# Shortening the first load of a DMA-bound max-pooling kernel from 8 KB to 2 KB per partition

## Chip, cores and metric

One core of one Trainium2 chip. The metric is the device time of one execution in microseconds (us); the span in a profile is about 1.8 us shorter.

The time of the kernel before was 335.2 us, the median of three runs (335.18 to 335.23).

## The reference

The input is 32 x 256 x 4096 fp32 (134.2 MB). Every window of 16 neighbours becomes its maximum; the output is 32 x 256 x 256 fp32 (8.4 MB).

```python
def reference(x, output_size):                 # x: (32, 256, 4096), output_size 256
    batch, channels, length = x.shape
    result = np.zeros((batch, channels, output_size), dtype=np.float32)
    for i in range(output_size):
        start = int(i * length / output_size)
        end = int((i + 1) * length / output_size)
        result[:, :, i] = np.max(x[:, :, start:end], axis=-1)
    return result
```

## The kernel before

The 2,097,152 windows are spread evenly: 16,384 to each of 128 partitions. They are loaded in pieces into three slots that are used in turn; VectorE reduces each piece. All results stay on chip in the same area, growing down from its top, so the slots must shrink as the results grow. The pieces form three groups. Within a group every partition has one contiguous row in HBM, and each group has its store; the last is cut in two.

```python
    AREA = 53200          # fp32 elements of a partition
    SLOTS = 3
    MOST = 65536 // (4 * W)      # 1024 windows: 64 KB of a partition; W = 16
    ALIGN = 4
    FIRST = 128           # windows of a partition in the first load
    ROUNDS_A = 3
    LAST = 4

    slot_sizes = [MOST]
    rounds = [[FIRST] + [MOST] * (SLOTS - 1)]
    left = total - sum(rounds[0])
    while left:
        room = AREA - (total - left)
        n = min(room // (SLOTS * W + SLOTS) // ALIGN * ALIGN, MOST)
        ...                                             # cut: fills `rounds`
    sizes = [n for r in rounds for n in r]
    groups = [sizes[:1], sizes[1 : ROUNDS_A * SLOTS], sizes[ROUNDS_A * SLOTS :]]
    ...                                                 # cut: views of input and output
        for i, size in enumerate(loads):
            a = b - size
            at = n_loads % SLOTS * slot_sizes[n_loads // SLOTS] * W
            slot = area[:, at : at + size * W]
            nc.sync.dma_start(out=slot, in_=xg[:, a * W : b * W])
            nc.vector.reduce_max(
                out=area[:, base + a : base + b],
                in_=slot.rearrange("p (n w) -> p n w", w=W),
                axis=mybir.AxisListType.X,
            )
            n_loads += 1
            b = a
    ...                                                 # cut: collects `stores`
    for dst, src in stores[1:2] + stores[0:1] + stores[2:]:
        nc.sync.dma_start(out=dst, in_=src)
```

So there are 20 loads and 4 stores, all issued in order by SyncE. The first three loads wait for nothing; each later load waits until the reduce of its slot's previous content has ended. The stores are, in order: second group, first group, most of the third group, and last the results of the last four reduces.

Of the kernel before, what the change touches and what calls it, by code (L numbers as in the profile page):

```python
# [1 line left out]

# [4 lines left out]


@with_exitstack
def kernel(  # L10
    ctx: ExitStack,
    tc: tile.TileContext,
    x: bass.AP,
    output_size: bass.AP,
    out: bass.AP,
):






    nc = tc.nc
    P = nc.NUM_PARTITIONS
    fp32 = mybir.dt.float32

    B, C, L = x.shape
    O = int(output_size)
    assert L % O == 0, (L, O)
    W = L // O  # L30
    total = B * C * O // P
    assert B * C * O % P == 0

    AREA = 53200
    SLOTS = 3
    MOST = 65536 // (4 * W)
    ALIGN = 4
    FIRST = 128
    ROUNDS_A = 3
    LAST = 4  # L40

# [7 lines that stand above are left out]
        if left <= slot_sizes[-1]:  # L49
            n = left  # L50
        slot_sizes.append(n)
        rounds.append([])
        while left and len(rounds[-1]) < SLOTS:
            n = min(n, left)
            rounds[-1].append(n)
            left -= n
    sizes = [n for r in rounds for n in r]
    groups = [sizes[:1], sizes[1 : ROUNDS_A * SLOTS], sizes[ROUNDS_A * SLOTS :]]

    pool = ctx.enter_context(tc.tile_pool(name="pool", bufs=1))  # L60
    area = pool.tile([P, AREA], fp32, tag="area", name="area")

    xw = x.flatten_outer_dims().rearrange("r (o w) -> (r o) w", w=W)
    ow = out.flatten_outer_dims().rearrange("r o -> (r o)")

    stores = []
    n_loads = 0
    first = 0
    low = AREA
    for g, loads in enumerate(groups):  # L70
        n = sum(loads)
        xg = xw[first : first + P * n].rearrange("(p n) w -> p (n w)", p=P)
        og = ow[first : first + P * n].rearrange("(p n) -> p n", p=P)
        first += P * n
        base = low - n
        b = n
# [12 lines that stand above are left out]
        low = base  # L89
        if g < len(groups) - 1:  # L90
            stores.append((og, area[:, base : base + n]))
        else:
            end = sum(loads[len(loads) - LAST :])
            for a, b in ((end, n), (0, end)):
                stores.append((og[:, a:b], area[:, base + a : base + b]))

    for dst, src in stores[1:2] + stores[0:1] + stores[2:]:
        nc.sync.dma_start(out=dst, in_=src)


# [1 line left out]
_INS = ['x', 'output_size']  # L102
_OUTS = [((32, 256, 256), 'float32')]

_NUMBERS = {'output_size': 256}


# [26 lines left out]
```

## Time and profile before

| What | Value | Where it is read |
|---|---|---|
| time, span | 335.2 us, 333.4 us | run times, page |
| DMA engines busy | 99.2% | queue section of the page |
| VectorE busy | 276.0 us (83%) | page, part 1 |
| VectorE's waits, all for loads | 49.2 us | view of waits |
| rate of 64 KB packets, one engine | 27.08 GB/s (2.42 us each) | packet records of the trace |

From the page of the kernel before:

```profile
span 333.4 us, 113 instructions
DVE 276.0 (83%) x20; POOL 0.2 (0%) x4
...
DMA packets 3456, 142.61 MB, mean 428 GB/s; under 512 B 384, under 2 KB 512, under 8 KB 512
...
q1 hardware_dynamic: 3456, 142.61, 99.2%
...
DMA 64%; DVE 31%; DVEq 1%; another core or an unknown queue 0%; SPq 0%; issue 0%
```

The line of queue q1 says that this one queue kept 16 engines busy for 99.2% of the span. The last line, the chain of waits, credits VectorE with 31%; a chain that meets a reduce just before a load's issue counts the reduce, even if the engines have another load queued meanwhile. The view of waits has, for VectorE (us in total, times, longest):

```profile
DVE area L82 <- DMA area<-in_x_dram: 49.2, 19, 17.1
```

The timeline of the kernel before (start us, duration, engine, line, operation, output<-input with shapes, count, and in brackets the idle time before and what ended it):

```profile
5.60 2.29 DVE L82 TENSOR_REDUCE area<-area 128x128 f32<-128x2048 f32 x1 [5.60 <-DMA area<-in_x_dram]
24.95 17.22 DVE L82 TENSOR_REDUCE area<-area 128x1024 f32<-128x16384 f32 x1 [17.06 <-DMA area<-in_x_dram]
44.30 17.22 DVE L82 TENSOR_REDUCE area<-area 128x1024 f32<-128x16384 f32 x1 [2.13 <-DMA area<-in_x_dram]
...
296.18 13.22 DVE L82 TENSOR_REDUCE area<-area 128x784 f32<-128x12544 f32 x1 [1.61 <-DMA area<-in_x_dram]
310.18 15.01 DVE L82 TENSOR_REDUCE area<-area 128x736 f32<-128x11776 f32 x2 [0.78 <-DMA area<-in_x_dram]
```

A reduce starts when its load has landed, and a load has landed when all of the 16 engines are done. The last line covers the last two reduces; they end at 310.18 + 15.01 = 325.19 us, when the last store can be issued.

### The profile page before, as it was taken

The numbers are of one execution on the slowest core, as the hardware profiler recorded it, in microseconds if no ns is written. First come the engines' busy times: TensorE is split into PE (matmuls) and PEld (weight loads), VectorE is DVE, ScalarE is ACT, GpSimd is POOL, SyncE is SP. The second block draws the span as 40 slices with busy tenths as digits, with TensorE's granted clock in tenths as the row PEclk, the third lists the DMA queues.
The fourth block names the chain that finished last, engine by engine and source line by source line (L and its number), as shares of the span: only waits on it lengthen the run. The fifth ranks groups of instructions, "written<-read, shape, count | busy, mean of one in ns | idle before, by whom it ended". The sixth has DMA issues, their size and how long they took to land.

```text
span 333.4 us, 113 instructions
## 1 busy us (share of the span) xinstructions
DVE 276.0 (83%) x20; POOL 0.2 (0%) x4
## 2 busy tenths in 40 slices
DVE  2009979797988989797989797989898898989990
POOL 0000000000000000000000000000000000000000
DMA  9898989898989998999999999999999999999997
GB/s 377 377 503 377 503 369 491 369 491 369 491 369 462 462 462 346 462 462 441 434 434 434 434 434 415 409 409 505 415 409 433 433 433 433 433 416 452 391 432 333
DMA packets 3456, 142.61 MB, mean 428 GB/s; under 512 B 384, under 2 KB 512, under 8 KB 512
## 3 DMA queue, kind: packets, MB, share of 16 engines
q1 hardware_dynamic: 3456, 142.61, 99.2%
HBM read 134.22 MB, written 8.39 MB: 428 GB/s over the span
## 4 chain that ended last, share of the span: by engine, by line
DMA 64%; DVE 31%; DVEq 1%; another core or an unknown queue 0%; SPq 0%; issue 0%
DMA area<-in_x_dram 64%; DVE area L82 31%; DVEq L129 1%; SPq L81 0%; DVEq L82 0%
## 5 line engine op out<-in xcount | busy, mean ns | idle before, releaser
L82 DVE TENSOR_REDUCE area<-area 128x1000 f32<-128x16000 f32 (+8 forms) x20 | 276.0, 13806 | 49.2 <-DMA area<-in_x_dram 49.2
L115 POOL MEMSET const-bfloat16-1.0<- 128x1 bf16 x1 | 0.1, 102 | 0.0
L115 POOL MEMSET const-uint8-127<- 128x1 uint8 x1 | 0.1, 102 | 0.0
L115 POOL MEMSET const-float32-0.0<- 128x1 f32 x1 | 0.1, 99 | 0.2 <-issue 0.2
L115 POOL MEMSET const-float32-1.0<- 128x1 f32 x1 | 0.1, 99 | 0.0
## 6 DMA issues: line engine op xcount, KB each, us to landing
area<-in_x_dram SPq DMA_DIRECT2D x3, 8000.0 KB, 39.9
area<-in_x_dram SPq DMA_DIRECT2D x3, 7520.0 KB, 37.5
area<-in_x_dram SPq DMA_DIRECT2D x3, 7072.0 KB, 35.3
area<-in_x_dram SPq DMA_DIRECT2D x3, 6656.0 KB, 33.2
area<-in_x_dram SPq DMA_DIRECT2D x3, 6272.0 KB, 31.3
area<-in_x_dram SPq DMA_DIRECT2D x1, 5888.0 KB, 30.3
out_dram<-area SPq DMA_DIRECT2D x1, 3934.0 KB, 27.4
out_dram<-area SPq DMA_DIRECT2D x1, 2966.0 KB, 33.7
```

The costliest lines, as they stand in the source:

```text
L82: nc.vector.reduce_max(out=area[:, base + a : base + b], in_=slot.rearrange("p (n w) -> p n w", w=W), axis=mybir.AxisListType.X,)
L115: nc = _bacc.Bacc("TRN2", target_bir_lowering=False, num_devices=1)
L129: with _tile.TileContext(nc) as tc:
```

## The change

The intent: the first load exists to give VectorE something early and to stagger the slots. A smaller one starts VectorE sooner and reads one contiguous quarter of a megabyte.

```diff
-    FIRST = 128
+    FIRST = 32
```

The arithmetic of the sizes moves the other 96 windows of each partition into the third group:

| | before | after |
|---|---|---|
| first load, elements of a partition | 2048 | 512 |
| third group's reduces, windows | 884 x3, 832 x3, 784 x3, 736, 152 | 888 x3, 836 x3, 784 x3, 740, 220 |
| first group's store, bytes of a partition | 512 | 128 |
| last two stores, elements of a partition | 5932, 2456 | 5956, 2528 |

The numbers of loads, stores and packets, and all bytes in total, stay the same.

## The prediction

> **What bounds the kernel now.** The DMA queue. The queue section of the page has 99.2% of 16 engines' span, 142.61 MB at 428 GB/s. The trace's DMA packet records show no gap from the first data packet (1.75 us into the span) to the last (332.1 us): 64 KB packets run at 27.08 GB/s per engine, and every load starts as the one before it ends. Outside that stream lie 1.7 us of start and 1.3 us of completion. VectorE is busy 276.0 us (83%); its 49.2 us of waits are all for loads (view of waits). The chain of waits names VectorE for 31%, but each load is issued with another one still queued ahead of it, so this costs nothing.
>
> **What the change does.** Total bytes, loads (20), stores (4) and packets stay. First load 2048 to 512 elements per partition, first reduce 128 to 32 windows; the 96 windows go into the third group: 884 to 888, 832 to 836 (three loads each), 736 to 740, the last 152 to 220. Stores: 128 to 32 windows (512 B to 128 B per partition), 5932 to 5956, 2456 to 2528.
>
> - First load: 8 packets per engine at 0.309 us become about 0.08 us each (estimate: 2 KB at 27.08 GB/s plus the few ns by which 8 KB packets exceed that rate): 1.8 us less. The later loads carry that: 1.8 us more. Net nil. The start-up of about 0.7 us (first packets take about 1 us, not 0.309) stays. The second load is issued 0.43 us after the first, which occupies the engines 0.6 us plus start-up: no hole.
> - Fourth load: issued at about 5 us instead of 7.9; worth nothing, as loads are queued until 44 us.
> - VectorE: a reduce fits 0.155 us + 1.041 ns per element of a partition. First 2.29 to 0.69 us; last 2.68 to 3.8; last but one 12.42 to 12.49.
> - Tail, the only place for a new wait: the last store is issued when the last reduce ends, 325.2 us, and its packets follow the third store's at 328.9 us without a gap; with about 1 us from issue to packets, some 2.5 us are slack. After: the last but one load lands about 1.3 us earlier (68 windows less before it), the two reduces take 1.2 us more: the last ends at 325.2 again.
> - Small store: now 0.2 to 0.3 us between its neighbours. The Trainium skill, "DMA: Bandwidth & Descriptors", Specifications, says that transfers under 512 B do a read-modify-write; nothing here shows it yet. Estimate: -0.1 to +0.3 us.
>
> On the critical path, nothing above 0.3 us changes.
>
> **Predicted: 335.2 us, 80% range 334.8 to 335.7. Faster by over 2%: 0.01; within 2%: 0.98; slower by over 2%: 0.01.**
>
> **What would show each step.** First reduce starts at about 3.8 us instead of 5.6; later reduces through the 784s 1.3 to 1.9 us earlier; the last ends at 325.2 within 0.3; DMA share stays 99%; 2 KB packets take 0.08 us once started; the third store's last packet and the fourth's first still touch.
>
> **What would make it wrong.** A hole at the start, if the second load's descriptors come after the short load's data end. 128 B store packets costing far more than 27 ns each. The third group's row pitch in HBM goes from 536,832 to 542,976 bytes: the same page (Latency and other measured facts) reports low rates at a 512 KiB pitch, restored by a few KiB more; before runs 12.25 KiB above that at full rate, after would run 18.25 KiB above, so I expect no loss, unproven here. The last reduce ending over 2 us late, which would expose the last store.

## The result, and the profile after

| | median us | range | runs |
|---|---|---|---|
| before | 335.19 | 335.16 to 335.23 | 6 |
| after | 335.56 | 335.24 to 335.85 | 6 |

The ratio is 1.001 (95% interval 0.9997 to 1.0023): the same within 2%, and inside the predicted range. A residue of some 0.4 us remains, and the runs scatter more than those of the kernel before.

The page of the kernel after (its profiled run took 335.85 us, the slowest of the six):

```profile
span 334.1 us, 113 instructions
DVE 276.0 (83%) x20; POOL 0.2 (0%) x4
...
DMA packets 3457, 142.61 MB, mean 427 GB/s; under 512 B 513, under 2 KB 513, under 8 KB 641
...
q1 hardware_dynamic: 3456, 142.61, 99.0%
...
DMA 64%; DVE 31%; DVEq 1%; another core or an unknown queue 0%; SPq 0%; issue 0%
```

Its timeline:

```profile
3.44 0.69 DVE L82 TENSOR_REDUCE area<-area 128x32 f32<-128x512 f32 x1 [3.44 <-DMA area<-in_x_dram]
23.76 17.22 DVE L82 TENSOR_REDUCE area<-area 128x1024 f32<-128x16384 f32 x1 [19.64 <-DMA area<-in_x_dram]
43.11 17.22 DVE L82 TENSOR_REDUCE area<-area 128x1024 f32<-128x16384 f32 x1 [2.13 <-DMA area<-in_x_dram]
...
295.43 13.22 DVE L82 TENSOR_REDUCE area<-area 128x784 f32<-128x12544 f32 x1 [1.61 <-DMA area<-in_x_dram]
309.51 16.21 DVE L82 TENSOR_REDUCE area<-area 128x740 f32<-128x11840 f32 x2 [0.86 <-DMA area<-in_x_dram]
```

VectorE does the same work in the same time (276.0 us), and its waits are 49.7 us instead of 49.2:

```profile
DVE area L82 <- DMA area<-in_x_dram: 49.7, 19, 19.6
```

The first reduce starts 2.16 us earlier, but the second only 1.19 us earlier, although the load ahead of it became 8 x 6144 B / 27.08 GB/s = 1.82 us shorter on every engine. So 0.63 us were lost between the first and the second landing. From the second reduce to the third the distance is 19.35 us in both kernels: nothing more is lost there. The last reduce ends at 309.51 + 16.21 = 325.72 us, 0.53 us later than before.

**Where the 0.63 us went.** The trace's packet records show it. In the kernel before, the first 64 KB packet of every engine took 2.42 us, like all later ones. In the kernel after these sixteen packets took 2.82 us on average, and one took 3.60 us. I define an engine's *lag* as follows: the time from the first data packet of the kernel to the end of that engine's last 64 KB packet, less what the same packets take at the steady rate (2.420 us for each 64 KB packet, and size / 27.08 GB/s + 5 ns for each packet of the first load). The 64 KB packets are those of the two full-size loads.

| | mean lag of 16 engines | lag of the slowest | fastest to slowest |
|---|---|---|---|
| before | 0.72 us | 0.91 us | 0.39 us |
| after | 0.88 us | 1.62 us | 1.06 us |

The excess arose in the long packets: when the first 64 KB packet of each engine began, the slowest engine lagged 0.73 us in the kernel after and 0.97 us in the kernel before. The other engines did not make the lag up: at the end of the kernel the engines' last data packets still end 1.04 us apart, against 0.44 us in the kernel before.

### The profile page after: what moved, and what is told of

It reads as the page before. It is cut to its first block, busy times and chain, and to the rows that moved or that the text cites. A ratio compares the mean times of both kernels' runs of the same rounds, so it can differ in the third digit from the quotient of the medians. Undisturbed runs are those within 1.5% of the kernel's fastest.

```text
span 334.1 us, 113 instructions
## 1 busy us (share of the span) xinstructions
DVE 276.0 (83%) x20; POOL 0.2 (0%) x4
## 4 chain that ended last, share of the span: by engine, by line
DMA 64%; DVE 31%; DVEq 1%; another core or an unknown queue 0%; SPq 0%; issue 0%
DMA area<-in_x_dram 64%; DVE area L82 31%; DVEq L129 1%; SPq L81 0%; DVEq L82 0%
## 5 line engine op out<-in xcount | busy, mean ns | idle before, releaser
L82 DVE TENSOR_REDUCE area<-area 128x1000 f32<-128x16000 f32 (+8 forms) x20 | 276.0, 13806 | 49.7 <-DMA area<-in_x_dram 49.7
```

What stands on the lines that cost most here:

```text
L82: nc.vector.reduce_max(out=area[:, base + a : base + b], in_=slot.rearrange("p (n w) -> p n w", w=W), axis=mybir.AxisListType.X,)
```

## The experiments

First theory, START: the residue arises in the first microseconds and the slowest engine carries it to the end. Its rival, REST: the residue comes from what the change did elsewhere, that is from the third group's new addresses or the 128 B store packets. All twelve kernels gave correct results, all in five rounds, on several chips; the kernel before was 335.1 to 335.5 us in every one of its runs beside them (medians 335.19 to 335.27). Diffs are against the changed kernel unless said otherwise.

### after_again: the changed kernel once more

No edit.

> The changed kernel unaltered, as a control for the small residue (335.56 us against 335.19, six runs each). If the residue is real: median 335.4 to 335.7 with runs spread over more than 0.3 us, where the kernel before stays within 0.1 us; and in the trace at least one of the second load's first sixteen 64 KB packets takes over 2.9 us instead of 2.42. If it was an accident of the first series: median 335.2 and a spread under 0.1 us.

Measured: 335.63 us (335.55 to 335.73, 5 runs) against 335.21 (335.11 to 335.29); ratio 1.0013, interval 1.0 to 1.0025. The longest first 64 KB packet took 3.28 us, the mean was 2.77. So the residue of 0.4 us came back and the two ranges do not overlap; the spread was smaller than expected, 0.18 us. I take it as real, and about a tenth of a per cent, though the interval just touches 1.

### short_fourth: the short load in the fourth place

```diff
-        for i, size in enumerate(loads):
-            ... load and reduce in group order ...
+    # pieces are collected first, then loaded and reduced in this order
+    for xg, base, a, b in state[1:4] + state[0:1] + state[4:]:
```

> The short load moves from first to fourth place; sizes, row pitches, stores and the 128 B packets stay as in the changed kernel. Theory START (the residue arises in the first microseconds, where the second load's 64 KB packets follow the short load's 2 KB packets before the engines run steadily, and the slowest engine keeps its lag to the end): median 335.1 to 335.3, spread under 0.15 us. Rival REST (the residue comes from the third group's new addresses or from the 128 B store packets): median 335.4 to 335.7 as in the changed kernel. Both expect VectorE's first reduce at about 22 us and no loss from that.

Measured: 337.89 us (337.59 to 338.20), slower than both expectations. I had built a new hole. The timeline of this kernel:

```profile
42.44 17.22 DVE L94 TENSOR_REDUCE area<-area 128x1024 f32<-128x16384 f32 x1 [2.10 <-DMA area<-in_x_dram]
61.35 17.41 DVE L94 TENSOR_REDUCE area<-area 128x1000 f32<-128x16000 f32 x2 [1.70 <-DMA area<-in_x_dram]
82.94 16.82 DVE L94 TENSOR_REDUCE area<-area 128x1000 f32<-128x16000 f32 x1 [4.18 <-DMA area<-in_x_dram]
```

The fifth load may be issued only when the reduce of the first line ends, at 59.66 us. Behind the third load there is now only the short one, 0.67 us of data, so the engines run dry: from 60.85 to 62.0 us only 7 to 14 of 16 engines are active, mostly 11 or 12, and the next reduce waits 4.18 us instead of some 2. The issue, from the timeline of 59 to 63 us:

```profile
59.68 0.33 SPq L93 DMA_DIRECT2D area<-in_x_dram  x1
```

The first packets of this late load (64,000 B) took 3.01 us on average instead of 2.36. So the run did not settle START against REST. But it showed that stretched first packets are not confined to the start of the kernel: they also come with a load that is issued too late in mid-stream.

### short_on_act: the short load from ScalarE's queue

```diff
-            nc.sync.dma_start(out=slot, ...)
+            (nc.scalar if n_loads == 0 else nc.sync).dma_start(out=slot, ...)
```

> Only the short load is issued by ScalarE's queue, so that the first long load no longer waits 0.43 us for the issue before it. Theory START by late issue (the long load's descriptors come after the 2 KB packets are done): the stretch of the first 64 KB packets (2.54 to 3.60 us in the changed kernel, mean 2.79) falls to under 0.15 us and the median to 335.2 or below. If the stretch has another cause than the issue gap, it stays and the median is 335.4 to 335.7. REST also expects 335.4 to 335.7.

Measured: 335.75 us (335.63 to 335.81). The test did not do what I meant. Both issues began in the same 0.01 us, but the packets of the short load came behind the first long packets: they ran from 3.1 us after the first data packet on, one between two long ones, and the last of them ended 21.6 us after it. The long load had become the first, its first packets took 3.09 us on average (2.82 in the kernel after, which the expectation has as 2.79), and the slowest engine lagged 1.58 us. The issue gap alone is thus not tested here.

### short_spread: the same 2 KB, from rows half a megabyte apart

```diff
-    groups = [sizes[:1], sizes[1 : ROUNDS_A * SLOTS], sizes[ROUNDS_A * SLOTS :]]
+    groups = [sizes[: ROUNDS_A * SLOTS], sizes[ROUNDS_A * SLOTS :]]
-            stores.append((og, area[:, base : base + n]))
+            for a, b in ((n - FIRST, n), (0, n - FIRST)):
+                stores.append((og[:, a:b], area[:, base + a : base + b]))
```

> The 2 KB of every partition come from the ends of the second group's rows, about half a megabyte apart, instead of one contiguous quarter megabyte; the small store is scattered likewise. If the contiguous quarter megabyte is what makes the start uneven: median 335.2 and no first 64 KB packet over 2.6 us. If only the size of the packets matters: median 335.4 to 335.7 with stretched first packets as in the changed kernel. REST expects 335.4 to 335.7 as well.

Measured: 335.89 us (335.75 to 335.97), longest first 64 KB packet 3.21 us, slowest engine's lag 1.48 us. The contiguous quarter of a megabyte is not the cause.

### first_16, first_64, first_512: other sizes of the first load

After these runs a second theory was formed, LEAD: a long load that the engines reach too soon after its issue has its first packets stretched, by different amounts on different engines; data queued ahead of it hides this. Its rivals are written in the expectations; one, SMALL, is that small packets at the very start leave the engines uneven, whatever follows.

```diff
-    FIRST = 32
+    FIRST = 16          # in the others 64 and 512
```

> First load of 1 KB per partition: half the lead of the changed kernel. LEAD expects the first 64 KB packets stretched more than there (mean over 2.8 us) and a median of 335.6 to 336.0. SMALL expects about the same as the changed kernel or more. REST (addresses of the third group) has no reason for a trend with the size.

> First load of 4 KB per partition, lead about 1.2 us plus start-up, between the two kernels of the case. LEAD expects first 64 KB packets with a mean between 2.42 and 2.77 us, and a median between those of the two kernels, 335.2 to 335.5.

> First load of 32 KB per partition: the other direction. DMA-bound view: total bytes are the same, so 335.2 again within 0.5 us. LEAD as far as it goes: the first load, longer itself, has no lead and its own first packets are stretched somewhat, so 335.2 to 335.7. If a longer first load cost time by starting VectorE later (first reduce at about 12 us): over 340 us.

Measured: 336.23 us (336.09 to 336.57) with 16 windows, 335.12 us (335.06 to 335.44) with 64, 335.25 us (335.22 to 335.31) with 512. The second reduce in the timelines of first_16 and of first_64, in this order:

```profile
24.12 17.22 DVE L82 TENSOR_REDUCE area<-area 128x1024 f32<-128x16384 f32 x1 [20.82 <-DMA area<-in_x_dram]
```

```profile
23.67 17.22 DVE L82 TENSOR_REDUCE area<-area 128x1024 f32<-128x16384 f32 x1 [18.40 <-DMA area<-in_x_dram]
```

With 64 windows the first load is 1.21 us shorter than with 128 (8 x 4096 B / 27.08 GB/s), and the second reduce starts 1.28 us earlier: nothing is lost. With 16 windows it is 2.12 us shorter, and the second reduce starts only 0.83 us earlier: 1.29 us are lost. The mean of the first 64 KB packets falls from 3.27 us (16 windows) over 2.82 (32) and 2.54 (64) to 2.42 (128). The trend is what LEAD says, though its medians were off: it forecast 335.6 to 336.0 us for 16 windows and 335.2 to 335.5 for 64. REST has no reason for it, and first_512, whose third group has other sizes and addresses again, is back at the time of before. Note that its first reduce starts only at 12.90 us, 7.3 us later than in the kernel before, which costs nothing.

first_64 is not faster than the kernel before: ratio 0.9999, interval 0.9987 to 1.0011. No version here beats both kernels.

### ladder: 2 KB, then 6 KB, then the long loads

Diff against the kernel *before*:

```diff
+            for c, d in ((0, 32), (32, size)) if n_loads == 0 else ((0, size),):
+                part = slot[:, c * W : d * W]
-                nc.sync.dma_start(out=slot, ...); reduce of the slot
+                nc.sync.dma_start(out=part, in_=xg[:, (a + c) * W : (a + d) * W]); reduce of the part
```

> The kernel before with its first load cut in two: 2 KB, then the other 6 KB of every row, then the long loads. New theory LEAD: a long load (64 KB per partition) that the engines reach less than about 2 us after its issue has its first packets stretched and uneven, because its packets are still being handed out; with more data queued ahead nothing is lost. LEAD expects here: the 6 KB packets in between give the lead back, first 64 KB packets 2.42 us (none over 2.6), median 335.1 to 335.4, spread under 0.2 us. Rival SMALL (2 KB packets in the first microsecond leave the engines uneven whatever follows): 335.5 or more and stretched 64 KB packets.

Measured: median 335.82 us (335.76 to 335.89, and one run of 337.27). LEAD was right about the long packets (mean 2.49 us, one of 2.75) and wrong about the time: the slowest engine lagged 1.59 us all the same, and the mean lag rose to 1.19 us. SMALL was right about the time and wrong about the long packets. Here the loss lies ahead of the long packets: in the first 0.9 us of data only about 8 of the 16 engines had a packet at any time (in the kernel after all 16 had one at 0.3 us), and the small packets moved 200 to 280 GB/s in the second microsecond, where the kernel before reached 424. Why half of the engines began late is not shown. LEAD is at best a part of the cause.

### short_second: the short load second, in a slot of its own

```diff
-    rounds = [[FIRST] + [MOST] * (SLOTS - 1)]
+    rounds = [[MOST] * SLOTS]          # the short load lies behind the three slots
+    # order: long, short, long, long; all four are issued at once
```

> The short load comes second, in a slot of its own, so that it and the long load behind it are issued at the start, some 20 us before the engines reach them. LEAD expects: the 2 KB packets at 0.084 us, the 64 KB packets behind them at 2.42 us (none over 2.6), no hole; only the very first long load, which has no lead, is stretched as when the short load went to ScalarE's queue; median 335.5 to 335.9. Rival SMALL/MID (a short load within the stream costs 2 to 3 us by itself, as the fourth place seemed to show with 337.89): median about 337 to 338.

Measured: 335.67 us (335.48 to 335.69). The 2 KB packets took 0.084 us each, and no hole followed. A short load in mid-stream is harmless if the load behind it is issued in time, so most of the 2.7 us that short_fourth lost, 2.2 us against this kernel, came with the late issue. Here a long load is first, its first packets took 3.10 us and the slowest engine lagged 1.37 us.

### third_late: only two loads issued in the first microsecond

```diff
+    for k in [0, 1, 3, 2] + list(range(4, len(state))):   # third and fourth load exchanged
```

> The changed kernel with its third and fourth load exchanged in the order of issue, so that the third issue waits for the first reduce (about 3.4 us after the first issue instead of 0.9 us) and only two loads are handed out in the first microseconds. Theory HANDOUT (the engines run under rate, and unevenly, as long as packets of all the loads issued back to back are being handed out; the cut first load, which made it four such loads, ended with 335.82): first 64 KB packets with a mean under 2.6 us, the engines' last 64 KB ends within 0.6 us of one another, median 335.3 or below. Theory LEAD (the second load itself was issued too shortly before the engines reach it; the third does not matter): mean 2.7 to 2.9 us, ends spread over 0.8 us, median 335.4 to 335.7.

Measured: 338.18 us (336.85 to 338.81). Issuing the third load 2.5 us later did nothing for the first 64 KB packets: mean 2.79 us. By that HANDOUT falls. Its second sign is not as clear: the engines' last 64 KB packets ended 0.62 us apart, between HANDOUT's forecast (under 0.6) and LEAD's (over 0.8), and the slowest engine lagged 1.24 us. The median is no evidence for either: the exchange left the sixth load with a slot that came free too late. Its timeline:

```profile
61.68 17.22 DVE L95 TENSOR_REDUCE area<-area 128x1024 f32<-128x16384 f32 x1 [2.52 <-DMA area<-in_x_dram]
78.93 18.90 SPq L94 DMA_DIRECT2D area<-in_x_dram  x3
80.66 16.82 DVE L95 TENSOR_REDUCE area<-area 128x1000 f32<-128x16000 f32 x1 [1.75 <-DMA area<-in_x_dram]
102.18 16.82 DVE L95 TENSOR_REDUCE area<-area 128x1000 f32<-128x16000 f32 x1 [4.71 <-DMA area<-in_x_dram]
```

SyncE issues again only at 78.93 us, when the reduce of the first line ends. The engines run dry (at 79.85 us only 4 of 16 are active), the sixteen first packets of this load took 3.28 us on average instead of 2.36, and the reduce after it waits 4.71 us.

### tail_half and tail_full: more VectorE work at the end

These test the prediction's slack at the end, and the 31% of the chain of waits. The last reduce (220 windows), or half of it, is done a second time before the last store.

```diff
+            if n_loads == len(sizes) - 1:
+                nc.vector.reduce_max(
+                    out=area[:, base + a : base + a + h],        # h = size // 2, or size
+                    in_=slot[:, : h * W].rearrange("p (n w) -> p n w", w=W), ...)
```

> The changed kernel with the first half (110 windows) of the last reduce done twice: about 1.99 us more of VectorE before the last store. The prediction's slack at the end is about 2.2 us here (last reduce ends at 325.7 us, first packets of the last store could come about 1 us after its issue, third store's packets end at about 329.0 us). Theory SLACK: no change, median 335.4 to 335.8. Rival CHAIN (VectorE at the end is on the critical path, as the chain of waits has it): median about 337.5.

> The changed kernel with the whole last reduce (220 windows) done twice: about 3.83 us more of VectorE before the last store. SLACK: the slack of some 2.2 us is used up and the rest shows: median 336.8 to 337.5, with a hole between the third and the fourth store's packets. CHAIN: about 339.4. If the end has far more slack than reckoned: 335.6.

Measured: 335.62 us (335.50 to 335.77) with half, 336.51 us (336.33 to 337.07) with the whole. The added reduces in the timelines of tail_half and of tail_full, in this order:

```profile
325.51 1.99 DVE L88 TENSOR_REDUCE area<-area 128x110 f32<-128x1760 f32 x1
```

```profile
325.58 3.82 DVE L88 TENSOR_REDUCE area<-area 128x220 f32<-128x3520 f32 x1
```

Two microseconds more of VectorE before the last store cost nothing (335.63 without, 335.62 with). Of 3.82 us, 0.88 us show: the slack of the slowest engine is about 2.9 us. The packet records of tail_full have the hole: the slowest engine ends the third store's packets at 329.5 us of the span and starts the fourth's at about 330.4. I had reckoned 2.2 us of slack, mostly because I took the average engine's end (329.0 us); the slowest one counts, and it ends later. Both times are far below what the chain of waits would have (337.5 and 339.4 us).

## Why the prediction was right, and where it was off

**Shown: one number accounts for the times.** The lag of the slowest engine, taken when the last 64 KB packet has landed, that is within the first fifth of the kernel, against the time of the same profiled execution:

| kernel | first 64 KB packets, mean us | mean lag | slowest lag | time us | time less slowest lag |
|---|---|---|---|---|---|
| before | 2.42 | 0.72 | 0.91 | 335.16 | 334.25 |
| first_64 | 2.54 | 0.63 | 0.96 | 335.11 | 334.15 |
| first_512 | 2.42 | 0.74 | 0.97 | 335.22 | 334.25 |
| tail_half | 2.96 | 0.80 | 1.23 | 335.62 | 334.39 |
| short_second | 3.10 | 0.91 | 1.37 | 335.67 | 334.30 |
| after_again | 2.77 | 0.87 | 1.39 | 335.63 | 334.24 |
| short_spread | 2.65 | 0.89 | 1.48 | 335.75 | 334.27 |
| short_on_act | 3.09 | 0.95 | 1.58 | 335.81 | 334.23 |
| ladder | 2.49 | 1.19 | 1.59 | 335.81 | 334.22 |
| after | 2.82 | 0.88 | 1.62 | 335.85 | 334.23 |
| first_16 | 3.27 | 1.18 | 2.32 | 336.57 | 334.25 |

The last column stays within 0.24 us while the times move by 1.46 us. Whatever follows the start costs all these kernels the same, whichever sizes, addresses and small stores they have. (Left out are tail_full, with its hole at the end, and the two kernels with a hole in mid-stream.) This is an account of where the time went, from one profiled execution of each kernel; it does not say what makes the lag. How much a single execution scatters is seen in after, after_again, tail_half and tail_full, which have the same start: their slowest lags are 1.62, 1.39, 1.23 and 1.45 us.

Point by point:

- *DMA alone bounds it, and the same bytes take the same time.* Right. The share of busy DMA engines was 99.0%, and the third group's packets of 47 KB and more ran at 27.01 to 27.05 GB/s at the new row pitch, 27.01 to 27.06 at the old.
- *An earlier VectorE is worth nothing.* Right: first reduces at 2.9 us (first_16) and 12.9 us (first_512) go with the slowest and with one of the fastest times.
- *2 KB packets take 0.08 us; the first reduce starts at about 3.8 us.* It was 0.084 us, and 3.44 us, a little earlier than forecast.
- *The end has slack.* Right, and tail_half shows it; its size was about 2.9 us for the slowest engine, not 2.5. In the kernel after, the fourth store's packets still follow the third's without a gap.
- *The small store costs between -0.1 and +0.3 us.* Right in effect: a 128 B packet took 13 ns, a 512 B packet 27 ns. The Trainium skill, "DMA: Bandwidth & Descriptors", Specifications, has a read-modify-write below 512 B; whether one took place cannot be seen here, and at 13 ns a packet no loss of note came of it.
- *The pitch in HBM.* No loss. The same page's Latency and other measured facts gives 207 GB/s at a 512 KiB pitch, hardly below the 214 GB/s that it calls full; its low rates, and the few KiB that restored one, belong to pitches of 2 MiB and more. The prediction had misread this. No run here has any of these pitches.
- *"The start-up of about 0.7 us ... stays ... no hole."* This is the step that was off, by a term of the sum. 0.7 us is the average engine's lag, and it went to 0.88; but the slowest engine decides, and its lag went from 0.91 to 1.62 us in the profiled run. An engine stood idle for only 0.06 us on average between the short and the long load, but the first long packets were stretched, from 2.42 to 2.82 us on average. The time was inside the range because the range had room for this 0.4 us, not because the start was foreseen. From this follow two more misses: the later reduces came 0.75 to 1.19 us earlier, not 1.3 to 1.9, and the last reduce ended at 325.72 us, not at 325.2 within 0.3.

**Not settled.** Why the start is uneven. What is shown is that the lag depends on what is in flight in the first two microseconds: small for first packets of 4, 8 and 32 KB, larger where 64 KB packets come first or behind 0.3 to 0.7 us of data, and larger with 2 KB and 6 KB in sequence. LEAD fits the sizes from 16 to 128 windows and the two late loads in mid-stream. The traces have its own quantity too, the time from the start of the long load's issue to its first packets, as a mean of 16 engines: 1.31 us in first_16, 1.48 in tail_half, 1.73 in after, 1.94 in short_spread, 2.34 in first_64 and 3.82 in before. In the same order those packets took 3.27, 2.96, 2.82, 2.65, 2.54 and 2.42 us; that is an order, not yet a cause. LEAD does not explain the ladder, whose long packets had 3.80 us and hardly stretched (2.49 us) while the lag was there before them, nor first_512, whose first packets were stretched too (1.84 us for 32 KB that take 1.21 us at the steady rate) but left the engines close together. SMALL alone does not do either, since a long load in first place (short_on_act, short_second) lags as well. The address theory (short_spread) fell, and so, by the first packets, did HANDOUT (third_late).

## What to carry to other kernels

Where the DMA queue never ran dry here, rearranging the same bytes moved nothing but the two ends; reckon each end for the slowest DMA engine, since a lag from the start was still there at the last store. Be wary of a first load so short that the engines reach the next long one soon after its issue: here 1.3 to 1.9 us after the issue began went with stretched packets and 0.4 to 1.0 us of time, and 2.3 us (first_64) with no loss. After any reordering check that each load is issued before the one ahead of it drains: two of these experiments lost 2.2 and some 2.5 us that way (short_fourth against short_second, third_late against after_again). Before believing a chain of waits that blames a compute engine, add work to that engine: here 2 us more cost nothing.

## What the Trainium skill lacked or had wrong

- "DMA: Bandwidth & Descriptors", Latency and other measured facts, gives about 600 ns to the first byte of such a DMA. The trace agrees: the first packet started 0.64 us after the end of the first issue. What that section lacks is how far apart such a start leaves the 16 engines: their lag differed by 0.39 us with 8 KB packets first, by 0.62 to 1.09 us in six runs with 2 KB packets ahead of 64 KB ones, and by 1.73 us with 1 KB packets, and before and after it was kept to the end (0.44 and 1.04 us there).
- The same section and page do not say that the first packets of a load that is issued too late are stretched: 3.01 and 3.28 us instead of 2.36 for 64,000 B in mid-stream.
- The same page, Specifications, has a read-modify-write under 512 B and line rate from 512 B up; that section gives no times for such packets. 128 B store packets took 13 ns each (9.8 GB/s) and 512 B ones 27 ns (19 GB/s), against 27.08 GB/s for 64 KB packets: the 128 B ones are slow as the page has it, but the 512 B ones are below line rate too. With eight per engine neither shows in the time.
- The same page, Bandwidth (Where 436 GB/s comes from), says that for transfers between HBM and SBUF a limit of about 358 GB/s binds. Taken alone, this does not hold here: only one core ran, and it moved 428 GB/s over the whole span. The table of the same section (425 GB/s for 16 MB) and "HBM Reference", Specifications, have it right for a core that streams alone (about 425 GB/s).
